# Fewer POOL taps in the second half's conv, more of its steps early, and weights split three chunks ahead

## The chip, the cores and the metric

The kernel runs on one core of one Trainium2 chip. The time is the device time of one launch in microseconds (us); before the change the median of three runs is 1130.25 us (1129.55 to 1130.99). Engines are called as in the profile: PE multiplies matrices, PEld loads its weights, DVE (vector), ACT (scalar, with function tables) and POOL (GpSimd) work elementwise, SP issues transfers. Each engine takes its instructions in one fixed order, and a waiting instruction holds those behind it.

## The reference, cut to what matters

Two layers on 512 tokens of 1024 channels. The change lies in the first, a conv module with an FFN behind it:

```python
a = jax.nn.glu(x @ w_pw1 + b_pw1, axis=-1)
y = lax.conv_general_dilated(
    a, w_dw[:, None, :].astype(a.dtype), window_strides=(1,),
    padding=((CONV_WIDTH - 1, 0),), dimension_numbers=('NWC', 'WIO', 'NWC'),
    feature_group_count=D_MODEL) + b_dw
y = jax.nn.silu(layernorm(y, ln_g, ln_b))
return y @ w_pw2 + b_pw2
```

So each channel of `a` is filtered with its own 31 taps over the current and the 30 tokens before it, the result is normalised over the channels and projected. The FFN is `(silu(gate) * up) @ w_down` on the RMS-normalised sum, with 2816 hidden channels. The second layer is windowed attention and another FFN, and a last norm follows.

## The kernel before, in words

Channels lie on the 128 partitions (8 channel tiles, KT), tokens along the free dimension. The first layer's conv is done in two halves of 256 tokens, so that the conv of one half, elementwise work, can run beside matmuls of the other.

**First projection** (`Pw1`, L555): for each half and channel tile 8 matmuls for the linear part and 8 for the gate, in fp32, each recorded as two. `gate` (L564 on ACT, L569 on DVE) writes the result to `a_pad`.

**Conv** (`Half.taps`, L594 to L608): the 31 taps of a channel tile are divided. N_POOL of them go the POOL way: ACT multiplies a shifted view by the tap (L594, L596) into one of 8 `pr` buffers, and POOL adds it to the running sum (L597). The others go the DVE way: a fused multiply and add into a PSUM bank (L602, L604), the last one into `y`. POOL then adds its sum to `y` (L608). Two channel tiles run side by side as a pair and share one PSUM bank; a step is one DVE tap of each with the POOL taps that fall to it. A pair with n POOL taps has 31 - n tap steps and one step that closes it. The halves have their own N_POOL, given by pair.

**Norm of the conv**: `squares` (DVE L631, ACT L633), `sums` (matmuls with ones, L642), `scales_a` (a copy on ACT, L647, small matmuls, L650, and four small DVE instructions, L652 to L657), `scales_b` (POOL L663, ACT L668), `spread` (PE L672), `rows` (DVE L684 and L685, ACT silu L686).

**Second projection and FFN** (`pw2`, `ffn_part`): their weights come as chunks of 128 x 1024 elements, one per `get`: 8 chunks of pw2, then 24 of the FFN's first part upwards and 12 downwards for one half of the tokens. A chunk is loaded into a `raw` buffer by SP (4 of them, six chunks ahead). The first half's pw2 uses it as it is, in fp32 (L253). All later chunks are split in `advance`: ACT rounds them to `whi` (L203), DVE subtracts for `wlo` (L204), and `mm3` does three matmuls for each pair of tiles (L255 to L257): 24 per chunk. Activations are split in the same way (L375 and L376 for the norm's input, L379 and L380 for the hidden layer). `whi` and `wlo` have 3 buffers each, and a chunk is split two gets ahead of its use. The FFN's RMS norm adds squares up on POOL (L333), sums them on PE (L343), takes the power on POOL (L347), makes a diagonal on ACT (L355) and spreads it on PE (L368). The first use of its result is the evacuation of hidden pairs (L454, L457 on DVE).

**Order.** The program is written as one sequence, and a planner puts each engine's instructions in order by its own estimate of times: of those that are ready in its estimate the one written first goes first. `issue_after(ins)` keeps what is traced inside it behind `ins` on the engine of `ins`. The second half's conv and norm is a generator (`Half.background`) that the first half's work drives: N_EARLY steps of it are taken in the 11th to 14th of the late projections (`at_` 10 to 13), and the rest is a job: `pace`, called in every `get`, takes as many steps as are due at that chunk, linearly over 42 chunks from the first half's second projection on. In the 12th projection (`at_` 11) the sums of the first half's last pair are traced behind the projection's matmuls.

Of the kernel before, what the change touches and what calls it, by code (L numbers as in the profile page):

```python
# [21 lines left out]
KT = D // P  # L22
# [11 lines left out]
HALVES0 = ((0, 6), (6, 11))  # L34
HALVES1 = ((0, 6), (6, 9))
LAST = (9, 11)
N_POOL = ((13, 13, 12, 12), (17, 17, 17, 17))

Q_HEADS = [g * 8 + s * 4 + j for g in range(2) for j in range(4) for s in range(2)]
HEAD_COLS = np.concatenate([np.arange(h * HD, (h + 1) * HD) for h in Q_HEADS])  # L40
# [109 lines left out]
def hybrid_trunk(ctx: ExitStack, tc: tile.TileContext, xT, W, prm_in, wdw_in, sinks, relb, onehot, outT):  # L150
    nc = tc.nc
    cpool = ctx.enter_context(tc.tile_pool(name="const", bufs=1))
    quads = ctx.enter_context(tc.tile_pool(name="quads", bufs=11))
    wpool = ctx.enter_context(tc.tile_pool(name="wts", bufs=3))
    tmp = ctx.enter_context(tc.tile_pool(name="tmp", bufs=5))
    small = ctx.enter_context(tc.tile_pool(name="small", bufs=4))
    ps = ctx.enter_context(tc.tile_pool(name="ps", bufs=8, space=PSUM))
# [8 lines left out]
    def bank():  # L166
        return ps.tile([P, 512], F32, tag="bank", name=uid("bank"))
# [4 lines left out]
    def temp():  # L172
        return tmp.tile([P, 512], F32, tag="tmp", name=uid("tmp"))
# [3 lines left out]

    stream = {"dma": 0, "split": 0, "use": 0}
    raws, splits = {}, {}
    DMA_AHEAD, SPLIT_AHEAD = 6, 2  # L180
    lo_engine = [nc.vector]

    def load(upto):
# [22 lines left out]

    jobs, background, rate, seen = [], [], [0], [0]

    def job(gen, n, g0, g1):
        jobs.append([gen, n, g0, g1, 0])  # L210

    def pace():
        g = seen[0] = seen[0] + 1
        for j in list(jobs):
            while j[4] < j[1] * (g - j[2]) / (j[3] - j[2]):
                j[4] += 1
                if next(j[0], "end") == "end":
                    jobs.remove(j)
                    break
# [17 lines left out]
    def get(*key):  # L237
        advance()
        pace()
        due[0] += rate[0]  # L240
        tick(int(due[0]))
        due[0] -= int(due[0])
        i = stream["use"]
        assert PLAN[i] == key, (PLAN[i], key)
        stream["use"] += 1
        hi, lo = splits.pop(i)
        n = {"kv": 4, "up": 4}.get(key[0], 2)
        sh = dict(a=n)
        return tuple(w and w.rearrange("p (a b) -> p a b", **sh) for w in (hi, lo))
# [53 lines left out]
    ones_m = cpool.tile([P, P], F32, tag="ones_m", name="ones_m")  # L303
# [220 lines left out]
    nc.gpsimd.memset(inv_s, -1.0 / 256)  # L524
    W2 = 256
    N_RAW = 2
    N_EARLY = (7, 3, 4, 2)
    raw = [x[:, HALF[1]] for x in xg]
    for i in range(KT):
        nc.vector.tensor_scalar(raw[i], h[i][:, HALF[0]], col("mix0", i), None, op0=ALU.mult)  # L530
# [3 lines left out]
    def norm_x(rms, tok, pb=None):  # L534
        pb = rms.spread() if pb is None else pb
        for i in range(KT):
            nc.vector.scalar_tensor_tensor(xg[i][:, tok], h[i][:, tok], col("mix0", i), pb,
                                           op0=ALU.mult, op1=ALU.mult)
        return pb

    with tc.tile_pool(name="conv", bufs=2) as cv:
# [29 lines left out]
        class Half:  # L571
            def __init__(self, hf, after=()):
# [3 lines left out]
                self.st = None  # L576
                self.n_steps = sum(TAPS - n + 1 for n in N_POOL[hf]) + KT + 7

            def taps(self, ct, c):
                n_pool = N_POOL[self.hf][ct // 2]  # L580
                a = a_pad[ct][:, self.hf * W2:(self.hf + 1) * W2 + PAD]
                yt = self.y[:, ct, :]

                def tap(j):
                    return wdw[:, ct, j:j + 1]

                nd = TAPS - n_pool
                acc, pi = None, 0
                for i in range(nd):
                    while pi * nd < n_pool * (i + 1):  # L590
                        j = nd + pi
                        pr = cv.tile([P, W2], F32, tag="pr", name=uid("pr"), bufs=8)
                        if acc is None:
                            on_act = nc.scalar.activation(pr, a[:, j:j + W2], AF.Identity, scale=tap(j), bias=col("bdw", ct))  # L594
                        else:
                            on_act = nc.scalar.mul(pr, a[:, j:j + W2], tap(j))  # L596
                            on_pool = nc.gpsimd.tensor_add(pr, acc, pr)  # L597
                        acc = pr
                        pi += 1
                    src = a[:, i:i + W2]  # L600
                    if i == 0 and ct < 4:
                        nc.vector.tensor_scalar(c, src, tap(i), None, op0=ALU.mult)  # L602
                    else:
                        on_dve = nc.vector.scalar_tensor_tensor(yt if i == nd - 1 else c, src, tap(i),  # L604
                                                                c if i else self.shift, op0=ALU.mult, op1=ALU.add)
                    yield
                self.last = on_act.ins, on_dve.ins, on_pool.ins
                nc.gpsimd.tensor_add(yt, yt, acc)  # L608
# [27 lines left out]
            def sums(self, p):  # L636
                if self.st is None:
                    self.st = bank()
                for e in range(2):
                    ct = 2 * p + e  # L640
                    for f, t in enumerate((self.y[:, ct, :], self.sq[e])):
                        nc.tensor.matmul(self.st[:, f * W2:(f + 1) * W2], ones_m, t,  # L642
                                         start=ct == 0 and f == 0, stop=ct == KT - 1 and f == 1)

            def scales_a(self):
                row = temp()
# [44 lines left out]
            def background(self):  # L691
# [3 lines left out]
                for p in range(KT // 2):  # L695
                    for s in range(TAPS - N_POOL[self.hf][p] + 1):
                        next(gen)
# [47 lines left out]
        h0 = Half(0)  # L745
        n_taps = sum(TAPS - n + 1 for n in N_POOL[0])
        taps = h0.conv()
# [20 lines left out]
        follow = {2: [rms1.step1, table_in], 4: [lambda: norm_x(rms1, HALF[1]), h0.shift_rows], 6: [table]}  # L768
        for p, at_ in enumerate((5, 7, 9, 10)):
            follow.setdefault(at_, []).append(lambda p=p: h0.squares(p))  # L770
            follow.setdefault(at_ + 1, []).append(lambda p=p: h0.sums(p))
        follow[11].append(h0.scales_a)
        done, early, late = 0, 0, None
        for at_, (hf, ct) in enumerate(projs):
            if at_ == 13:
                with tc.issue_after(proj.last[1]):
                    spread = h0.spread()
            with tc.issue_after(spread) if at_ == 13 else nullcontext():
                proj = Pw1(hf, ct)
            if late is not None:  # L780
                with tc.issue_after(proj.last[0]):
                    late.gate()
                    gated = late.sig
            late = proj if hf else None
            if hf == 0:
                proj.gate()
                last_sig = proj.sig
            while done < n_taps * min(1, (at_ + 1) / 11):
                next(taps, None)
                done += 1  # L790
            for f in follow.get(at_, ()):
                with tc.issue_after(last_sig) if f is table else nullcontext(), tc.issue_after(proj.last[1 if f == h0.scales_a or at_ < 11 else 0]):
                    f()
            if at_ == 10:
                h1 = Half(1, h0.last)
                second = h1.background()
            if at_ >= 10:

                with ExitStack() as st:
                    for ins in (gated, h0.copied if at_ == 11 else None, h0.varied if at_ == 11 else None, h0.spreads if at_ >= 12 else None):  # L800
                        if ins is None:
                            continue
                        st.enter_context(tc.issue_after(ins))
                    for _ in range(N_EARLY[at_ - 10]):
                        next(second)
                        early += 1
            if at_ == 11:
                h0.scales_b()
# [3 lines left out]
            late.gate()  # L812
        h1.after = [h0.silu]
        base = seen[0]
        job(second, h1.n_steps - early, base, base + 42)
        x0 = {"ffn0": Act(KT)}
        bc0 = new_bc()
        n0 = Next(("ffn0",), x0, bc0, HALF[0])
# [8 lines left out]
    def read_bias():  # L827
        for h0_ in range(0, NH, 2):
            yield
            nc.sync.dma_start(bias[:, h0_:h0_ + 2, :],  # L830
                              bass.AP(tensor=fd.tensor, offset=fd.offset + 127 + h0_ * 3 * P,
                                      ap=[[NH * 3 * P - 1, P], [3 * P, 2], [1, BAND]]))

    base = seen[0]
    job(read_bias(), 9, base, base + 30)
    n1 = Next(("ffn0",), x0, bc0, HALF[1])
    pw2(h1.z, n1)
    ffn_part(0, 0, x0["ffn0"], HALF[1], n1.rms)
# [11 lines left out]
    if True:  # L850
# [20 lines left out]
        for half in range(2):  # L871
# [7 lines left out]
            if half == 0:  # L879
                rs_bc = rms.step2()  # L880
                rs = rms.rs
                for m in range(2):
                    t = temp()
# [4 lines left out]
        for n in range(4):  # L888
            t = temp()
# [258 lines left out]
```

## Time and profile before

| | before |
|---|---|
| median of three runs | 1130.25 us |
| profiled execution | 1130.66 us |
| its span in the trace | 1128.9 us |
| granted TensorE clock, mean | 0.996 |
| busy: PE | 1103.1 us (98%) |
| busy: PE's weight loads | 960.1 us (85%) |
| busy: DVE | 660.7 us (59%) |
| busy: ACT | 515.0 us (46%) |
| busy: POOL | 334.6 us (30%) |

The span is the profiled execution from its first to its last instruction; 1.76 us of its own time lie around it. Busy shares are means over the whole span; the stages differ. In the trace the second projection of the first half begins at 131.3 us, its FFN at 161.35 us, and the second half's own projection and FFN follow from about 265 us. Rows of groups give the line, engine, operation, shapes and count, then the busy time, the mean of one in ns, and the idle time just before with what ended it.

### The profile page before, as it was taken

To read this page: it belongs to the slowest core of one execution; us is meant where nothing else is said; L and a number is where in the kernel's file an instruction comes from. 1 tells how busy PE (TensorE), PEld (TensorE's weight loads), DVE (VectorE), ACT (ScalarE), POOL (GpSimd) and SP (SyncE) were. 2 spreads that over 40 slices of the span, in tenths; PEclk is the share of its full clock that TensorE was granted. 3 is DMA by queue.
4 is the path that set the end of the run, shared out by engine and by line. 5 is a ranking of instruction groups with operands and counts; after the bars stand their busy time and mean duration, and the time that the engine had idled before them with its cause. 6 is when DMAs were issued, how large, how long until landed. Compare 5 with 4: busy or idle time off the path is not lost.

```text
span 1128.9 us, 16125 instructions
## 1 busy us (share of the span) xinstructions
PE 1103.1 (98%) x6140; PEld 960.1 (85%) x6140; DVE 660.7 (59%) x1060; ACT 515.0 (46%) x910; POOL 334.6 (30%) x437
## 2 busy tenths in 40 slices
PE   8999998899999999999999999999999999999997
PEld 7888887899999998888888777888888888888886
DVE  4998868877765554444464685764454333444355
ACT  3886787856454432332352564653232221222234
POOL 3999699930010001111220232231121100110014
PEclk9999999999999999999999999999999999999998
DMA  9227053466555552323223211123223322232222
GB/s 357 100 31 83 23 181 114 137 204 223 184 179 180 187 167 98 106 91 96 93 85 102 76 38 38 38 61 108 93 93 99 106 94 94 93 100 103 96 96 92
DMA packets 41722, 128.16 MB, mean 114 GB/s; under 512 B 4491, under 2 KB 12844, under 8 KB 41644
## 3 DMA queue, kind: packets, MB, share of 16 engines
q1 hardware_dynamic: 40924, 126.56, 35.7%
q8 instruction: 48, 0.79, 0.3%
q10 hardware_dynamic: 720, 0.57, 0.2%
q14 instruction: 30, 0.25, 0.1%
HBM read 121.87 MB, written 5.24 MB: 113 GB/s over the span
## 4 chain that ended last, share of the span: by engine, by line
PE 85%; DVE 5%; issue 5%; POOL 2%; ACT 2%; DMA 1%; SPq 0%; POOLq 0%; ACTq 0%; DVEq 0%
PE bank L255 24%; PE bank L256 24%; PE bank L257 24%; PE bank L555 8%; POOL pr L597 2%; PE bank L919 1%; DVE bank L604 1%; PE bank L940 1%; DVE quad L376 1%; PE bank L642 1%; DVE wlo L204 1%; ACT whi L203 1%; DMA h<-in_xT_dram 1%; ACT pr L596 0%; DVE sc L922 0%
## 5 line engine op out<-in xcount | busy, mean ns | idle before, releaser
L257 PE MATMUL bank<-quad,wlo 128*128 128x512 f32 (+1 forms) x1584 | 542.4, 343 | 4.5 <-DVE wlo L204 4.5
L256 PE MATMUL bank<-quad,whi 128*128 128x512 f32 (+1 forms) x1584 | 542.6, 343 | 2.4 <-DVE quad L376 2.4
L255 PE MATMUL bank<-quad,whi 128*128 128x512 f32 (+1 forms) x1584 | 542.7, 344 | 0.8 <-ACT whi L203 0.6
L204 DVE TENSOR_TENSOR wlo<-raw,whi 128x1024 fp32r<-128x1024 f32 x200 | 271.4, 1357 | 326.0 <-ACT whi L203 317.6
L203 ACT CAST whi<-raw 128x1024 fp32r<-128x1024 f32 x200 | 209.6, 1048 | 357.8 <-PE bank L256 306.5
L257 PEld LDWEIGHTS bank<-quad,wlo 128*128 128x128 f32 x1584 | 299.9, 189 | 40.4 <-DVE wlo L204 6.0
L256 PEld LDWEIGHTS bank<-quad,whi 128*128 128x128 f32 x1584 | 300.2, 189 | 38.2 <-DVE quad L376 3.4
L255 PEld LDWEIGHTS bank<-quad,whi 128*128 128x128 f32 x1584 | 300.0, 190 | 37.1 <-ACT whi L203 0.8
L465 POOL TENSOR_TENSOR tmp<-tmp,tmp 128x512 f32<-128x512 f32 x32 | 45.6, 1427 | 485.0 <-DVE tmp L464 471.5
L597 POOL TENSOR_TENSOR pr<-pr,pr 128x256 f32<-128x256 f32 x220 | 170.5, 812 | 14.0 <-ACT pr L596 13.7
L596 ACT ACTIVATE pr<-apad,wdw 128x256 f32<-128x256 f32 x220 | 105.3, 503 | 27.1 <-POOL pr L597 25.3
L555 PE MATMUL bank<-quad,w 128*128 128x256 f32 x512 | 113.4, 380 | 2.3 <-DMA w<-in_W_dram 1.3
L555 PEld LDWEIGHTS bank<-quad,w 128*128 128x128 f32 x512 | 96.6, 190 | 17.3 <-DVE quad L530 4.1
L604 DVE SCALAR_TENSOR_TENSOR bank<-apad,wdw,bank 128x256 f32<-128x256 f32 x236 | 108.5, 485 | 3.6
L333 POOL TENSOR_TENSOR tmp<-tmp,tmp 128x256 f32<-128x256 f32 (+1 forms) x42 | 44.4, 1057 | 133.4 <-ACT tmp L329 109.4
L463 ACT ACTIVATE tmp<-tmp 128x512 f32<-128x512 f32 x32 | 20.1, 632 | 86.4 <-DVE tmp L462 86.4
L933 POOL TENSOR_SCALAR sc<-sc,sm 128x256 f32<-128x256 f32 (+1 forms) x64 | 30.8, 503 | 86.1 <-DVE sm L931 86.0
L379 ACT CAST quad<-tmp 128x512 fp32r<-128x512 f32 (+1 forms) x48 | 27.9, 585 | 29.7 <-POOL tmp L465 25.8
L376 DVE SCALAR_TENSOR_TENSOR quad<-h,prm,quad 128x512 fp32r<-128x512 f32 (+1 forms) x40 | 39.2, 1011 | 1.9 <-ACT quad L375 1.7
L464 DVE TENSOR_TENSOR tmp<-bank,rsbc 128x512 f32<-128x512 f32 x32 | 22.1, 691 | 30.4 <-PE bank L257 30.4
L929 ACT ACTIVATE sc<-sc,m 128x257 f32<-128x257 f32 (+1 forms) x64 | 30.2, 475 | 15.2 <-DVE m L922 14.5
L380 DVE TENSOR_TENSOR quad<-tmp,quad 128x512 fp32r<-128x512 f32 (+1 forms) x48 | 31.0, 650 | 2.3 <-ACT quad L379 2.3
(137 smaller groups left out, 749.7 us busy)
## 6 DMA issues: line engine op xcount, KB each, us to landing
raw<-in_W_dram SPq DMA_DIRECT2D x208, 512.0 KB, 3.5
w<-in_W_dram SPq DMA_DIRECT2D x15, 512.0 KB, 9.6
fd<-fs SPq DMA_DIRECT2D x1, 3072.0 KB, 33.8
h<-in_xT_dram SPq DMA_DIRECT2D x8, 256.0 KB, 6.6
bias<-fd SPq DMA_DIRECT2D x8, 256.0 KB, 7.8
out_dram<-res SPq DMA_DIRECT2D x13, 128.0 KB, 1.8
w<-in_W_dram SPq DMA_DIRECT2D x2, 256.0 KB, 4.4
out_dram<-res ACTq DMA_DIRECT2D x3, 128.0 KB, 2.4
```

The costliest lines, as they stand in the source:

```text
L203: nc.scalar.copy(hi, r)
L204: lo_engine[0].tensor_sub(lo, r, f32(hi))
L255: nc.tensor.matmul(out, w[0], x[0], start=start, stop=False)
L256: nc.tensor.matmul(out, w[0], x[1], start=False, stop=False)
L257: nc.tensor.matmul(out, w[1], x[0], start=False, stop=stop)
L333: self.eng.tensor_add(sq, self.acc, sq)
L376: nc.vector.scalar_tensor_tensor(dst[1], src, g, f32(dst[0]), op0=ALU.mult, op1=ALU.subtract)
L465: nc.gpsimd.tensor_mul(t2, t1, t2)
L555: mm = nc.tensor.matmul(self.pb[:, w * W2:(w + 1) * W2], w1[ct][:, w, k, :], x[k] if x else xg[k][:, tok], start=k == 0, stop=k == KT - 1)
L596: on_act = nc.scalar.mul(pr, a[:, j:j + W2], tap(j))
L597: on_pool = nc.gpsimd.tensor_add(pr, acc, pr)
L604: on_dve = nc.vector.scalar_tensor_tensor(yt if i == nd - 1 else c, src, tap(i), c if i else self.shift, op0=ALU.mult, op1=ALU.add)
```

## The change

Four edits. In the second half's conv the pairs 2 to 4 have 15 POOL taps instead of 17, so 16 DVE taps instead of 14. The four late projections take 8, 4, 5 and 3 steps of that conv instead of 7, 3, 4 and 2, and the job's due steps are now a broken line: 20 steps within the first 8 chunks (the second projection), the rest evenly up to chunk 42. The sums of the first half's last pair are traced between the linear and the gate half of the 12th projection, and the gate half is kept behind them. Weights are split three gets ahead instead of two, with 4 buffers for `whi` and `wlo` each.

```diff
-N_POOL = ((13, 13, 12, 12), (17, 17, 17, 17))
+N_POOL = ((13, 13, 12, 12), (17, 15, 15, 15))
...
-    wpool = ctx.enter_context(tc.tile_pool(name="wts", bufs=3))
+    wpool = ctx.enter_context(tc.tile_pool(name="wts", bufs=4))
...
-    DMA_AHEAD, SPLIT_AHEAD = 6, 2
+    DMA_AHEAD, SPLIT_AHEAD = 6, 3
...
-    def job(gen, n, g0, g1):
-        jobs.append([gen, n, g0, g1, 0])
+    def job(gen, *points):
+
+        jobs.append([gen, points, 0])
+
+    def due_at(points, g):
+        for (g0, n0), (g1, n1) in zip(points, points[1:]):
+            if g <= g1:
+                return n0 + (n1 - n0) * (g - g0) / (g1 - g0)
+        return 1 << 30
...
-            while j[4] < j[1] * (g - j[2]) / (j[3] - j[2]):
-                j[4] += 1
+            while j[2] < due_at(j[1], g):
+                j[2] += 1
...
-    N_EARLY = (7, 3, 4, 2)
+    N_EARLY = (8, 4, 5, 3)
...
-        follow[11].append(h0.scales_a)
+        follow[11] = [h0.scales_a]
...
-                proj = Pw1(hf, ct)
+                proj = Pw1(hf, ct, mid=(lambda: h0.sums(3)) if at_ == 11 else None)
...
-        job(second, h1.n_steps - early, base, base + 42)
+        job(second, (base, 0), (base + 8, 20), (base + 42, h1.n_steps - early))
...
-    job(read_bias(), 9, base, base + 30)
+    job(read_bias(), (base, 0), (base + 30, 9))
```

`sums` now returns its last matmul, behind which `Pw1` puts the gate half (`with tc.issue_after(mid()) if w and mid`); the bias job keeps its line.

More of the change, by code (lines that the diff above doesn't have):

```diff
@@ L641, in sums @@
                     for f, t in enumerate((self.y[:, ct, :], self.sq[e])):
-                        nc.tensor.matmul(self.st[:, f * W2:(f + 1) * W2], ones_m, t,
-                                         start=ct == 0 and f == 0, stop=ct == KT - 1 and f == 1)
+                        mm = nc.tensor.matmul(self.st[:, f * W2:(f + 1) * W2], ones_m, t,
+                                              start=ct == 0 and f == 0, stop=ct == KT - 1 and f == 1)
+                return mm.ins
             def scales_a(self):
```

## The prediction

> **What bounds the kernel now.** I began with the page's busy times and slices.
>
> ```profile
> span 1128.9 us, 16125 instructions
> ...
> PE 1103.1 (98%) x6140; PEld 960.1 (85%) x6140; DVE 660.7 (59%) x1060; ACT 515.0 (46%) x910; POOL 334.6 (30%) x437
> ...
> POOL 3999699930010001111220232231121100110014
> ```
>
> PE bounds the program; only stretches in which PE waits can give time back. POOL is full in slices of 28 us between about 28 and 240 us and nearly idle afterwards, and that is where the conv lies that the change edits. So I read next what PE waited for from 150 to 480 us: waits in total, their number, the longest.
>
> ```profile
> PE bank L257 <- DVE wlo L204: 4.5, 5, 1.3
> PE bank L368 <- ACT tmp L355: 1.8, 1, 1.8
> PE bank L256 <- DVE quad L376: 1.5, 2, 0.9
> PE bank L343 <- POOL tmp L333: 1.1, 1, 1.1
> PE bank L650 <- ACT tmp L647: 0.7, 1, 0.7
> PE bank L255 <- ACT whi L203: 0.6, 1, 0.6
> ```
>
> All but the 0.7 fall between 161 and 240 us, beside the first half's FFN: 9.5 us in 10 waits. A wait costs a little more than its idle time:
>
> ```profile
> 214.91 0.28 PE L255 MATMUL bank<-quad,whi 128*128 128x256 f32 x1
> 215.03 0.28 PE L256 MATMUL bank<-quad,whi 128*128 128x256 f32 x1
> 216.31 0.39 PE L257 MATMUL bank<-quad,wlo 128*128 128x256 f32 x1 [0.99 <-DVE wlo L204]
> ```
>
> Neighbours start 0.12 us apart, here it is 1.28: 1.16 us are lost for 0.99 idle. With 0.17 us for each of the 10, the stage loses **11.2 us**; that is all this stage can give. A weight chunk of 24 matmuls is 24 x 0.12 = 2.88 us of PE.
>
> Why is the weight split (L203 on ACT, then L204 on DVE) late? The chain of waits just before the last of these stalls (start, us, what):
>
> ```profile
> 219.68 1.58 issue
> 221.26 0.73 POOL pr L597
> ...
> 222.07 2.42 POOL pr L597 x2
> ...
> 224.94 1.04 ACT whi L203
> ...
> 226.01 1.68 DVE wlo L204
> ...
> 227.73 0.39 PE bank L257
> ```
>
> The chain runs along POOL's tap additions, over to ACT and DVE, and so to PE. ACT's queue is in order: a product (L596) that waits for one of eight `pr` buffers, which only POOL's addition frees, holds the split queued behind it. From 161.4 to 240 us:
>
> ```profile
> ACT pr L596 <- POOL pr L597: 10.5, 16, 1.9
> DVE wlo L204 <- ACT whi L203: 9.4, 9, 1.9
> ```
>
> POOL has no gap between 138.61 and 233.7 us. Ahead of that it has two (timeline of POOL: start, us, count, idle before):
>
> ```profile
> 116.15 2.79 POOL L597 TENSOR_TENSOR pr<-pr,pr 128x256 f32<-128x256 f32 x4 [4.37 <-ACT pr L596]
> ...
> 119.58 9.68 POOL L597 TENSOR_TENSOR pr<-pr,pr 128x256 f32<-128x256 f32 x14
> ...
> 138.61 10.73 POOL L597 TENSOR_TENSOR pr<-pr,pr 128x256 f32<-128x256 f32 x15 [7.99 <-ACT pr L596]
> ```
>
> **POOL's work, and what the change takes from it.** An undisturbed addition is 9.68/14 = 0.69 us. In the full stretch (groups from 138.6 to 233.8 us; POOL, then DVE):
>
> ```profile
> L597 POOL TENSOR_TENSOR pr<-pr,pr 128x256 f32<-128x256 f32 x94 | 83.4, 921 | 8.3 <-ACT pr L596 8.0
> ```
> ```profile
> L204 DVE TENSOR_TENSOR wlo<-raw,whi 128x1024 fp32r<-128x1024 f32 x21 | 33.4, 1592 | 15.6 <-ACT whi L203 15.6
> ```
>
> The 94 took 83.4 - 94 x 0.69 = 18.5 us more than undisturbed, while DVE did 21 wlo subtractions: 0.88 us for each. Where POOL is idle (280 to 400 us) the subtraction itself is shorter:
>
> ```profile
> L204 DVE TENSOR_TENSOR wlo<-raw,whi 128x1024 fp32r<-128x1024 f32 x42 | 51.3, 1224 | 36.3 <-ACT whi L203 36.1
> ```
>
> So each makes the other wait, and POOL's loss goes with the number of splits, not with the number of additions.
>
> The change drops from 17 to 15 POOL taps for six of eight channel tiles: 12 additions and 12 products fewer, 12 more DVE taps. The early steps (N_EARLY) rise from 16 to 20. The first pair of tiles takes 15 steps, so five steps of the second pair come early instead of one: 10 products and 8 additions instead of 4 and 2. Those 6 additions can run in the gaps of 4.37 and 7.99 us. The stretch loses 18 additions: 18 x 0.69 = **12.4 us**; ends: 12 x 0.69 = 8.3 us if the early ones find no room, 18 x 0.92 = 16.6 us if each is worth the mean. I take 0.69 since the splits that lengthen the others remain. The Trainium skill, "SBUF — State Buffer", section "Who interferes with whom", states that a VectorE instruction with two SBUF inputs and a GpSimd instruction that reads SBUF hold one shared port by turns, each for its whole length, while one SBUF input does not contend. By that rule 12.4 stands (L204 reads two SBUF tiles, a tap one tile and a PSUM bank); by the group's mean alone it would be 16.6. The trace agrees with the rule: 1.22 against 1.59 us for L204.
>
> Is POOL then early enough? Before, 59 job steps are spread over 42 chunks, and the last tap step is the 44th: chunk 31.3, that is 23.3 after the 8 of the second projection. the FFN starts here:
>
> ```profile
> 161.35 0.47 PE L255 MATMUL bank<-quad,whi 128*128 128x256 f32 x1
> ```
>
> PE reaches the last tap step at 161.35 + 23.3 x 2.88 = 228.5 us if nothing stalls; POOL is done at 233.7, about 5 us late. After, 20 steps come in the first 8 chunks and the last tap step is the 46th: chunk 8 + 26 x 34/41 = 29.6, PE at 222.7 us; POOL at 233.7 - 12.4 = 221.3. It is **no longer late**. Splitting three chunks ahead, with a fourth pair of buffers, adds cover: a split is asked for one chunk, 2.88 us, earlier, and the longest split wait is 1.3. The split waits (4.5 + 0.6 us in 6 waits, 6.1 with the restarts) should mostly go.
>
> **DVE is the next.** Busy times by stage (us; PE, PEld, DVE, ACT, POOL):
>
> ```profile
> 131.30:161.35 30.05, 30.05 (x141) 26.43 (x141) 18.22 (x40) 23.89 (x51) 22.74 (x31) 1.00 0.38 122
> 161.35:190.00 28.65, 24.20 (x186) 22.92 (x185) 24.81 (x39) 21.83 (x46) 28.65 (x31) 1.00 0.45 149
> 190.00:237.30 47.30, 42.07 (x328) 39.95 (x328) 42.38 (x60) 38.43 (x68) 43.41 (x46) 1.00 0.45 148
> ```
> ```profile
> L604 DVE SCALAR_TENSOR_TENSOR bank<-apad,wdw,bank 128x256 f32<-128x256 f32 x48 | 23.1, 481 | 0.6
> ```
>
> In the FFN's 75.95 us DVE has 67.2 us of work (88%). Without stalls the same PE work takes 75.95 - 11.2 = 64.8 us, so DVE would be the bound there unless work leaves the stage. In program order 52 of 112 taps were due by the end of the second projection; after, 76 of 124. So 48 instead of 60 remain: 12 x 0.481 = 5.8 us less, and one split (1.59) falls earlier: 59.8 of 64.8 us. The 24 taps that move need 11.5 us, and DVE has 30.05 - 18.22 = 11.8 us free beside the second projection. It just fits, so I don't expect all of the 6.1 us back: I take 70%, **4.3 us**; ends 2.0 and 6.1. On ACT 12 products fewer are no gain of their own; its waits are POOL's.
>
> **The other terms.** The sums of the first half's last pair move between the two halves of the 12th projection. Now PE does 32 matmul records, then the sums, then waits:
>
> ```profile
> 106.19 7.07 PE L555 MATMUL bank<-quad,w 128*128 128x256 f32 x32
> 113.09 0.59 PE L642 MATMUL bank<-y,ones_m 128*128 128x256 f32 x2
> ...
> 115.66 1.05 PE L650 MATMUL bank<-ident,tmp 128*128 128x1 f32 x8 [0.68 <-ACT tmp L647]
> ```
> ```profile
> 106.75 0.40 ACT L633 ACTIVATE sq<-y 128x256 f32<-128x256 f32 x1
> ```
>
> The squares are done at 107.15; half of the projection ends at 106.19 + 6.9/2 = 109.6. So the sums run 3.45 us earlier, the copy (L647) is hidden behind the projection's other half, and the wait with its restart, **0.8 us**, goes; ends 0 and 0.8. Four early steps more are 8 DVE taps ahead of the first half's normalised rows, but DVE ran taps of those very steps there already, and it idles 5.43 us while PE does the sums:
>
> ```profile
> 116.75 0.16 DVE L652 TENSOR_SCALAR mv<-bank 128x2 f32<-128x2 f32 x1 [5.43 <-PE bank L650]
> ```
>
> So I let the rows move with PE. The first four waits of the FFN (1.8 + 1.5 + 1.1 us, 5.1 with restarts) are start-up: the norm's sum on POOL, its scale, the split of x on DVE. One wlo subtraction fewer stands among the x splits; I take **0.6 us** off, ends -2.5 (a loss) and +2.5, because the planner may order these queues anew. After 480 us PE's longest wait is the tail's, and none is for a weight split (L203, L204):
>
> ```profile
> PE bank L1072 <- DVE tmp L1062: 1.5, 1, 1.5
> PE bank L256 <- DVE ptl L944: 1.3, 2, 0.7
> ```
>
> So three chunks ahead bring nothing there; the new orders are worth 0, ends 0.6 either way. Raw loads get no slower: one buffer less is held between load and split.
>
> Sum: 0.8 + 4.3 + 0.6 = 5.7 us. The profiled execution took 1130.66 us (1128.9 in the span, 1.76 around it), so it would take 1125.0; it stands 0.41 above the median of the three runs, 1130.25, for which I say **1124.5 us**.
>
> **Rivals.** *A, DVE takes POOL's place.* If the third pair of tiles gets no PSUM bank for its sums before the second projection ends (before, DVE stood idle there in a gap of 6.20 us although taps were left), the 24 taps don't move: DVE's stage load is 67.2 + 5.8 - 1.6 = 71.4 us, and at 94% density that is 76 us, what the stage takes now. Only the 0.8 us stay: 1129.5. The row that speaks for it:
>
> ```profile
> 156.69 1.64 DVE L204 TENSOR_TENSOR wlo<-raw,whi 128x1024 fp32r<-128x1024 f32 x1 [6.20 <-ACT whi L203]
> ```
>
> Against it: the third pair's first step is the 13th of the job instead of the 15th, and at 20 steps in 8 chunks it is asked for at chunk 6 instead of 11.
> *B, slower: the norm's sum queues behind the pulled-forward taps.* POOL does 31 operations beside the second projection. After the change 47 are due there if the early ones find no room: the second pair's 30, 14 of the third, 3 of the norm (L333). The 16 left behind may stand ahead of the four L333 that complete the FFN's norm, the last of which runs here:
>
> ```profile
> 177.41 0.72 POOL L333 TENSOR_TENSOR tmp<-tmp,tmp 128x256 f32<-128x256 f32 x1
> ```
>
> Six tap additions stand between those four now, so 10 are new: 10 x 0.92 = 9.2 us in which PE waits at L343. It decides once that last L333 ends more than 6 us later than now against the FFN's start; fully paid it gives 1124.5 + 9.2 = 1133.7. Against it: 8 of the 16 fit the gaps of 4.37 and 7.99 us, and the additions interleave with taps today at equal load.
> *C, all stalls go:* 0.8 + 11.2 = 12 us, 1118.2. Against it: the start-up chain POOL, DVE, ACT, PE is a dependence, not a queue alone.
>
> **Chances.** Forecast 0.62, A 0.18, B 0.09, C 0.11. A measurement can tell about 0.2% (2.3 us) from no change. The forecast's own range by the ends is 0.8 + 2.0 - 2.5 - 0.6 to 0.8 + 6.1 + 2.5 + 0.6, near 0 to 10 us, mostly over 2.3; so faster 0.58 of 0.62 plus C plus a little of A: 0.72; same 0.20; slower 0.08, nearly all B. The range, 1119.5 to 1131.5, takes in the forecast, A and the milder part of C.
>
> **What would show it.** Right: no 0.7 wait at L650; POOL's full stretch ends near 221 us and ACT's waits for `pr` fall well under 10.5; PE's waits for wlo fall from 4.5 to about 1; DVE's gap of 6.20 is filled with taps. Wrong: POOL still full until 230 us (12.4 mis-sized), DVE over 95% in the FFN with PE waiting on L204 or L376 (A), or PE's wait at L343 or L368 grown by several us (B).

## The result, and the profile after

The changed kernel takes 1122.53 us (median of five runs, 1121.57 to 1123.15), the kernel before 1129.66 us on the same chip. The ratio is 0.9929 with a 95% interval of 0.9918 to 0.9941: between 0.6% and 0.8% faster. The forecast was 1124.5. The profiled execution took 1122.53 us, its span is 8.2 us shorter. Three rows of its page:

```profile
span 1120.7 us, 16124 instructions
...
PE 1103.7 (98%) x6140; PEld 963.7 (86%) x6140; DVE 663.5 (59%) x1072; ACT 509.2 (45%) x898; POOL 324.0 (29%) x425
...
POOL 3999699810200001211230232241111100110014
```

POOL has 12 instructions fewer and DVE 12 more, and POOL's slices between about 170 and 250 us read 9, 8, 1 instead of 9, 9, 3. (Seven lines were added ahead of the conv, so L255 to L257 are now L262 to L264, L333 is L340, L343 is L350, L368 is L375, L376 is L383, L597 is L604, L604 is L611, L608 is L615, L642 is L649; with one more, L647 is L655 and L650 is L658.) What PE waits for from 150 to 480 us, the view that had six rows and 10.2 us:

```profile
PE bank L350 <- POOL tmp L340: 3.1, 1, 3.1
PE bank L263 <- DVE quad L383: 0.9, 3, 0.4
```

All waits for weight splits are gone (5.1 us before), so are the waits for the spread of the norm's scale (1.8) and for the copy of the conv's sums (0.7). One wait has grown, from 1.1 to 3.1 us: that for the FFN norm's sum. And something new stands behind it. PE's timeline there (start, us, operation, idle before):

```profile
178.58 0.61 PE L350 MATMUL bank<-ones_c,tmp 128*128 128x1 f32 x4 [3.10 <-POOL tmp L340]
...
179.36 0.28 PE L264 MATMUL bank<-quad,wlo 128*128 128x256 f32 x1
179.48 0.28 PE L262 MATMUL bank<-quad,whi 128*128 128x256 f32 x1
...
180.22 0.42 PE L264 MATMUL bank<-quad,wlo 128*128 128x256 f32 x1
180.44 0.41 PE L262 MATMUL bank<-quad,whi 128*128 128x256 f32 x1
```

From 0.12 us apart the same matmuls go to 0.22. The windows' column of the granted clock (the third from the right) tells why:

```profile
179.90:183.30 3.40, 3.40 (x18) 3.40 (x18) 1.37 (x3) 2.20 (x4) 3.40 (x5) 0.50 0.35 102
```

For 3.41 us TensorE runs at half its clock, which costs about 1.7 us. In the profiled execution of the kernel before there was no such stretch in this stage.

POOL's timeline has the gap at 111 to 116 us closed, and the full stretch now runs from 139.42 to 219.6 us, 80.2 us instead of 95.1:

```profile
105.78 12.42 POOL L604 TENSOR_TENSOR pr<-pr,pr 128x256 f32<-128x256 f32 x18
...
139.42 9.83 POOL L604 TENSOR_TENSOR pr<-pr,pr 128x256 f32<-128x256 f32 x14 [9.59 <-ACT pr L603]
...
192.81 26.80 POOL L604 TENSOR_TENSOR pr<-pr,pr 128x256 f32<-128x256 f32 x27
```

The groups in that stretch, POOL and then DVE:

```profile
L604 POOL TENSOR_TENSOR pr<-pr,pr 128x256 f32<-128x256 f32 x76 | 69.1, 943 | 9.6 <-ACT pr L603 9.6
```
```profile
L204 DVE TENSOR_TENSOR wlo<-raw,whi 128x1024 fp32r<-128x1024 f32 x18 | 27.9, 1548 | 10.3 <-ACT whi L203 10.2
```

94 additions became 76. What the additions take beyond 0.69 us comes to (69.1 - 76 x 0.69) / 18 = 0.93 us per split, 0.88 before. The trace shows directly that it is paid per split: sorted by what DVE did at the same time, the 31 additions that overlap a split (L204) take 1.22 us on average, and the 38 that overlap neither a split nor the split of x (L383) take 0.73 us, none of them more than 0.75 (0.69 from start to start).

### The profile page after: what moved, and what is told of

The parts are those of the page before. It is cut to its first block, busy times and chain, and to the rows that moved or that the text cites. A ratio compares the mean times of both kernels' runs of the same rounds, so it can differ in the third digit from the quotient of the medians.

```text
span 1120.7 us, 16124 instructions
## 1 busy us (share of the span) xinstructions
PE 1103.7 (98%) x6140; PEld 963.7 (86%) x6140; DVE 663.5 (59%) x1072; ACT 509.2 (45%) x898; POOL 324.0 (29%) x425
## 4 chain that ended last, share of the span: by engine, by line
PE 90%; DVE 3%; ACT 3%; issue 2%; POOL 1%; DMA 1%; POOLq 0%; SPq 0%; ACTq 0%; DVEq 0%
PE bank L262 26%; PE bank L263 26%; PE bank L264 25%; PE bank L562 9%; PE bank L927 1%; PE bank L649 1%; PE bank L948 1%; ACT pr L603 1%; POOL pr L604 1%; DVE quad L383 1%; ACT whi L203 1%; DVE wlo L204 0%; DVE bank L611 0%; DVE sc L930 0%; DMA raw<-in_W_dram 0%
## 5 line engine op out<-in xcount | busy, mean ns | idle before, releaser
L262 PE MATMUL bank<-quad,whi 128*128 128x512 f32 (+1 forms) x1584 | 543.8, 345 | 0.2
L264 PE MATMUL bank<-quad,wlo 128*128 128x512 f32 (+1 forms) x1584 | 542.9, 343 | 0.0
L204 DVE TENSOR_TENSOR wlo<-raw,whi 128x1024 fp32r<-128x1024 f32 x200 | 269.3, 1347 | 318.2 <-ACT whi L203 310.1
L262 PEld LDWEIGHTS bank<-quad,whi 128*128 128x128 f32 x1584 | 300.7, 190 | 36.5 <-ACT quad L966 0.6
L264 PEld LDWEIGHTS bank<-quad,wlo 128*128 128x128 f32 x1584 | 300.9, 190 | 34.5 <-DVE wlo L204 0.2
L604 POOL TENSOR_TENSOR pr<-pr,pr 128x256 f32<-128x256 f32 x208 | 160.5, 822 | 11.0 <-ACT pr L603 11.0
L611 DVE SCALAR_TENSOR_TENSOR bank<-apad,wdw,bank 128x256 f32<-128x256 f32 x248 | 113.2, 485 | 3.5
L562 PEld LDWEIGHTS bank<-quad,w 128*128 128x128 f32 x512 | 98.5, 193 | 14.9 <-DVE quad L537 0.9
L603 ACT ACTIVATE pr<-apad,wdw 128x256 f32<-128x256 f32 x208 | 99.6, 503 | 23.8 <-POOL pr L604 21.7
L340 POOL TENSOR_TENSOR tmp<-tmp,tmp 128x256 f32<-128x256 f32 (+1 forms) x42 | 45.2, 1076 | 135.2 <-ACT tmp L336 111.1
L383 DVE SCALAR_TENSOR_TENSOR quad<-h,prm,quad 128x512 fp32r<-128x512 f32 (+1 forms) x40 | 39.4, 1020 | 0.5 <-ACT quad L382 0.4
```

The costliest lines, as they stand in the source:

```text
L204: lo_engine[0].tensor_sub(lo, r, f32(hi))
L262: nc.tensor.matmul(out, w[0], x[0], start=start, stop=False)
L264: nc.tensor.matmul(out, w[1], x[0], start=False, stop=stop)
L340: self.eng.tensor_add(sq, self.acc, sq)
L383: nc.vector.scalar_tensor_tensor(dst[1], src, g, f32(dst[0]), op0=ALU.mult, op1=ALU.subtract)
L562: mm = nc.tensor.matmul(self.pb[:, w * W2:(w + 1) * W2], w1[ct][:, w, k, :], x[k] if x else xg[k][:, tok], start=k == 0, stop=k == KT - 1)
```

## The experiments

The prediction's theory, called L in the expectations, is that PE waits for splits because POOL is late and ACT's order hands that on. Twelve kernels were run. "Only" means the kernel before with one part of the change; "without" means the changed kernel with one part taken back. Beside the ratio to the kernel before I give two sums from each profile: PE's idle time between 95 and 270 us, and the time at half clock ahead of the tail. Both come from one execution of each kernel.

| kernel | ratio (95%) | PE idle, us | half clock, us |
|---|---|---|---|
| before | 1 | 11.0 | 0 |
| changed | 0.9929 (0.9918 to 0.9941) | 4.0 | 3.4 |
| only the taps | 0.9986 (0.9976 to 0.9995) | 8.3 | 6.8 |
| only the splits | 0.9981 (0.9972 to 0.9991) | 7.9 | 3.4 |
| only the steps | 1.0022 (1.0012 to 1.0032) | 11.1 | 10.2 |
| without the splits | 0.9959 (0.9944 to 0.9974) | 6.0 | 3.4 |
| without the taps | 0.9971 (0.9960 to 0.9982) | 6.7 | 3.4 |
| without the steps | 0.9944 (0.9928 to 0.9960) | 5.4 | 3.4 |
| without the moved sums | 0.9950 (0.9935 to 0.9965) | 5.5 | 3.4 |
| norm's additions on DVE | 0.9934 (0.9919 to 0.9949) | 4.7 | 3.4 |
| norm's sum a chunk later | 0.9958 (0.9943 to 0.9973) | 5.7 | 3.4 |
| last two squares summed by PE | 0.9945 (0.9928 to 0.9961) | 4.8 | 3.4 |
| last four squares summed by PE | 0.9945 (0.9931 to 0.9960) | 3.7 | 3.4 |
| norm ahead of the taps | 0.9907 (0.9891 to 0.9924) | 3.1 | 3.4 |

The half clock doesn't come equally often in every execution. The mean granted clock of the kernel before is 0.994 in ten of the 25 runs beside the first experiments and 0.996 or 0.997 in the rest; its profile has 0.996 with 8.4 us of half clock, all in the tail. A mean of 0.994 takes over 12 us of it, so by this estimate those ten had a stretch earlier too. And each edit makes the planner order all engines anew; no run here changes one part and keeps the order, so how much of a difference of 1 or 2 us is the part and how much the order stays open.

**Only the taps.**

```diff
-N_POOL = ((13, 13, 12, 12), (17, 17, 17, 17))
+N_POOL = ((13, 13, 12, 12), (17, 15, 15, 15))
```

> The kernel before with only the POOL taps of pairs 2 to 4 changed from 17 to 15 (12 additions fewer on POOL, 12 taps more on DVE). Theory L (PE's waits for weight splits are POOL's lateness, handed on by ACT's order): POOL's full stretch, 138.6 to 233.7 us, ends some 8 us earlier (12 x 0.69), the waits of PE for wlo and whi fall from 5.1 us to 1 to 2, and the time falls by about 4 us, to 1126. Theory S (the split is simply asked for too late; POOL's load matters little): the waits for wlo stay between 4 and 5 us and the time stays within 1 us of before.

Less than half of the 4 us expected by L: 0.14%, 1.6 us. POOL's stretch ends at 226.4 us, 7.4 us earlier, as L says. PE's waits from 95 to 270 us:

```profile
PE bank L257 <- DVE wlo L204: 2.4, 3, 1.1
PE bank L642 <- POOL y L608: 2.2, 1, 2.2
...
PE bank L255 <- ACT whi L203: 0.4, 1, 0.4
```

The split waits fell from 5.1 to 2.8 us as L says, though not to 1 or 2. But a wait of 2.2 us for POOL's last addition of a pair (L608) is new. It is the third pair's: with more tap steps it closes later, at 211.3 us instead of 201.1, and the planner puts its sums (L642) later too, but not by as much (290 weight-split matmuls behind the FFN's start instead of 242, and 48 are 5.8 us at 0.12). And two stretches at half clock appear, some 3.4 us lost, which neither theory had.

**Only the splits.**

```diff
-    wpool = ctx.enter_context(tc.tile_pool(name="wts", bufs=3))
+    wpool = ctx.enter_context(tc.tile_pool(name="wts", bufs=4))
...
-    DMA_AHEAD, SPLIT_AHEAD = 6, 2
+    DMA_AHEAD, SPLIT_AHEAD = 6, 3
```

> The kernel before with only the splits three chunks ahead and four buffers for whi and wlo. Theory L: POOL is late as before (full until about 231 us), one chunk of cover (2.88 us) takes about half of the 6.1 us of split waits: about 3 us faster, 1127. Theory S: all split waits go: 6 us faster, 1124, with POOL's stretch still as full as before.

```profile
PE bank L257 <- DVE wlo L204: 3.3, 6, 1.1
PE bank L650 <- ACT tmp L647: 2.0, 2, 1.3
PE bank L343 <- POOL tmp L333: 1.7, 1, 1.7
PE bank L256 <- DVE quad L376: 0.9, 2, 0.6
```

These are PE's waits from 95 to 270 us in this kernel. By the medians it is 2.2 us faster. S falls: with one chunk more of cover, 3.3 of the 5.1 us of split waits stay. L's "about half" was a little too much.

**Only the steps.**

```diff
...
-    N_EARLY = (7, 3, 4, 2)
+    N_EARLY = (8, 4, 5, 3)
...
-        job(second, h1.n_steps - early, base, base + 42)
+        job(second, (base, 0), (base + 8, 20), (base + 42, h1.n_steps - early))
```

(`job` and `pace` change with it, as in the whole diff.)

> The kernel before with only the earlier steps (8, 4, 5, 3 beside the late projections, then 20 within the first 8 chunks). Theory L: about 6 additions move out of the full stretch, 4 us less on POOL there, about 2 us faster; the gap of 6.2 us on DVE at 150 to 157 us is filled. Theory S: no change within 1 us. If pulled-forward taps delay the FFN's norm, PE's wait for POOL before the norm's sum grows from 1.1 us to 3 or more, and the time stays or grows.

L's 2 us of gain didn't come: 2.2 us slower by the medians, with an interval wholly above 1. PE's waits, and two windows behind the longest of them:

```profile
PE bank L649 <- POOL y L615: 3.8, 1, 3.8
PE bank L264 <- DVE wlo L204: 3.0, 3, 1.2
PE bank L375 <- ACT tmp L362: 1.8, 1, 1.8
PE bank L350 <- POOL tmp L340: 1.5, 1, 1.5
```
```profile
222.00:224.90 2.90, 0.99 (x9) 0.78 (x7) 2.81 (x3) 0.34 (x1) 2.90 (x2) 1.00 0.26 78
224.90:231.80 6.90, 5.00 (x21) 4.82 (x22) 2.52 (x3) 2.77 (x5) 2.53 (x4) 0.51 0.41 135
```

Not the norm's sum (1.5 us) but the conv's last sums are what PE waits for here, 3.8 us. POOL ends the first of that pair's last additions at 226.7 us, 12 us earlier than before (238.6), but the planner puts the sums 386 weight-split matmuls behind the FFN's start instead of 576, and 190 matmuls are 23 us at 0.12. The 10.2 us at half clock cost about 4.2 us, since PE stood idle in 1.8 of them. A part of a change that helps in company costs time alone.

**Without the splits, without the taps, without the steps.** Each is one of the three diffs above, taken back from the changed kernel.

> The changed kernel with splits two chunks ahead and three buffers, as before. Theory L (POOL no longer late, so the cover is hardly used): at most 1 us slower than the changed kernel, 1123 to 1124, PE's waits for wlo under 1 us. Theory J (fewer taps and earlier steps only set the stage, and PE's order is written for a POOL that real time doesn't follow; the extra chunk is what absorbs that): waits for wlo or whi of 3 to 5 us return, 1126 to 1128.

> The changed kernel with 17 POOL taps in all pairs. Theory L: POOL's stretch is full until about 228 us again, about 4 us slower than the changed kernel, 1126 to 1127, and PE waits for POOL's last addition of a pair (y) or for wlo. Additive reading of the runs so far (taps alone gave 1.6 us): 1124.

> The changed kernel with the old early steps (7, 3, 4, 2) and the old even pace. Additive reading (the steps alone cost 2.2 us): 2 us faster than the changed kernel, 1120. If the steps matter because DVE has 12 taps more and needs the room beside the second projection (rival A of the prediction): PE waits for wlo or for sums, 1126 or more, DVE idle again for some 5 us between 150 and 157 us.

Without the splits PE waits 1.9 us for wlo and whi again and at both ends of the norm's chain; the ratio is higher by 0.0030 (3.4 us), its interval just above the changed kernel's. That is a larger loss than L's 1 us, with less than J's 3 to 5 us of waits. Without the taps the loss is the largest, 0.42% (0.9971 against 0.9929), 4.7 us, near L's 4:

```profile
PE bank L350 <- POOL tmp L340: 3.5, 1, 3.5
PE bank L264 <- DVE wlo L204: 1.5, 2, 1.1
PE bank L658 <- ACT tmp L655: 1.2, 1, 1.2
```
```profile
197.17 30.24 POOL L604 TENSOR_TENSOR pr<-pr,pr 128x256 f32<-128x256 f32 x30
227.37 1.44 POOL L615 TENSOR_TENSOR y<-y,pr 128x256 f32<-128x256 f32 x2
```

POOL is full until 227.4 us, as L said (228). But with POOL as late as that only 1.5 of the 5.1 us of split waits are back, and the profiled execution, at 1124.86 us, is the fastest of this kernel's seven: it and one more (1125.07) have a mean clock of 0.996, the other five take 1126.1 to 1127.7 us at 0.992 or 0.993. So part of the 4.7 us goes with more time at half clock. Without the steps the interval overlaps the changed kernel's: no loss can be told, and no gain, so the additive reading falls. DVE does stand idle beside the second projection there, but PE's waits for wlo are only 0.4 us:

```profile
154.50 1.62 DVE L204 TENSOR_TENSOR wlo<-raw,whi 128x1024 fp32r<-128x1024 f32 x1 [5.52 <-ACT whi L203]
```

**Without the moved sums.** The sums of the first half's last pair stand behind the whole 12th projection again.

```diff
-        follow[11] = [h0.scales_a]
+        follow[11].append(h0.scales_a)
...
-                proj = Pw1(hf, ct, mid=(lambda: h0.sums(3)) if at_ == 11 else None)
+                proj = Pw1(hf, ct)
```

> The changed kernel with the sums of the first half's last pair behind the whole projection, as before. By the prediction's term: PE's wait at the copy of the sums (0.68 us, 0.8 with the restart) comes back at about 115 us, 0.8 us slower than the changed kernel, 1123.3. If the earlier sums also set the early steps going (they wait for the copy), POOL's pause of 4.4 us at 112 to 116 us comes back too and POOL ends later: 1 to 3 us slower.

The wait of 0.68 us is back and POOL's pause at 115 us with 3.0 us, but POOL's stretch ends no later (219.3 us, 219.6 in the changed kernel), which the second case had expected; the ratio rises by 0.0021, but the intervals overlap, so its size stays open between nothing and some 4 us.

**The wait that has grown.** Five kernels tried to remove the 3.1 us at the norm's sum.

```diff
...
+                self.rms.eng = self.eng or nc.gpsimd
...
+        n0.eng = nc.vector
```

> The changed kernel with one edit more: the additions of squares for the first half's FFN norm (7 of 128x256) run on DVE instead of POOL. If PE's wait of 3.1 us at the norm's sum is POOL's queue, it falls under 1 us; if the 3.41 us at half the TensorE clock that follow are a consequence of that wait, they go as well: 3.1 + 1.7, about 4 to 5 us faster than the changed kernel, 1118. If the granted clock falls for another reason, the half-clock stretch stays and the gain is 3 us at most. If DVE's load is the limit there, PE waits for x (quad) or wlo instead, and the time stays at about 1122.

Here the norm's additions (L340) run on DVE. No wait at the sum is left, yet the time is the changed kernel's: PE waits 2.3 us for x (L383), 1.3 for wlo and 1.0 for the spread, and a half-clock stretch comes at 170.3 us.

```diff
+                    if half == 0 and which == 0 and pending:
+                        rms.step1()
...
             if w == 256 and pair == lo:
-                rms.step1()
```

> The changed kernel with the FFN norm's sum on PE traced one chunk (2.88 us) later, for both halves. If the 3.1 us wait at that sum is only its place in PE's order, it falls to about 0.5 us, and if the half-clock stretch after it follows from the wait, that goes too: 3 to 4 us faster than the changed kernel, 1118 to 1119. If the norm's chain (POOL, DVE, POOL, ACT, PE) is what everything behind it depends on, the wait comes back at the spread of the scale (ACT tmp) and the time stays within 1 us of 1122.

The wait moved, as the second case says, but the time didn't stay within 1 us: 1124.62 us, with an interval (0.9943 to 0.9973) just above the changed kernel's. 0.3 us are left at the sum, and then

```profile
PE bank L375 <- ACT tmp L362: 4.6, 1, 4.6
```

The chain of waits shows what the scale's power (L354) waits for: POOL does conv additions (L605 in this kernel) between the norm's last addition and the power.

```profile
181.40 0.60 issue
182.00 0.09 POOL pr L605
...
183.40 1.73 POOL pr L605
...
186.43 0.72 POOL pr L605
187.16 1.66 POOL rs L354
...
188.84 0.04 ACT tmp L362
...
189.59 1.22 PE bank L375 x2
```

The next two leave the last two, or four, of the eight squares to PE's sum.

```diff
-            for i in range(n):
-                nc.tensor.matmul(st[:, i:i + 1], self.acc[:, i * P:(i + 1) * P], ones_c, start=i == 0, stop=i == n - 1)
+            parts = [self.acc] + self.rest
+            for a, part in enumerate(parts):
+                for i in range(n):
+                    nc.tensor.matmul(st[:, i:i + 1], part[:, i * P:(i + 1) * P], ones_c,
+                                     start=a == 0 and i == 0, stop=a == len(parts) - 1 and i == n - 1)
...
+        n0.n_sum = 6
```

> The changed kernel, in which the last two of the eight squares of the first half's FFN norm aren't added up by POOL but go to PE's sum as they are (4 small matmuls more, 0.5 us on PE; 2 additions fewer on POOL). If PE's wait of 3.1 us at the sum is the last two additions' place in POOL's queue, it falls below 1 us and the half-clock stretch after it goes: 3 to 4 us faster than the changed kernel, 1119. If the power on POOL and the diagonal behind it hold the chain, the wait comes back at the spread (ACT tmp): within 1 us of 1122.5.

> The same with the last four squares (8 small matmuls more, 1 us on PE; 4 additions fewer on POOL, which then has only the tap additions of this stretch in its queue ahead of the power). Queue reading: no wait at the sum, the power comes earlier as well, a gain of 3 to 4 us, 1119. Chain reading: the wait at the spread stays, 1122 to 1123.

No wait at the sum is left in either, but with two squares 3.9 us came back at the spread, with four 1.3 us there and 1.3 us at a wlo. Neither gains: 1124.07 and 1124.25 us. So with two squares it is POOL's queue ahead of the power that PE waits for: the planner puts 14 conv additions between the norm's last addition and the power, 6 in the changed kernel. The last kernel therefore fixes POOL's order itself: no conv step is due in the FFN's first four chunks, and later additions are kept behind the norm's last addition and behind the power.

```diff
+    hold = []
...
                 rms.step1()
+                for a in hold:
+                    a.append(rms.power)
+                hold.clear()
...
+        hold.append(h1.after)
...
-        job(second, (base, 0), (base + 8, 20), (base + 42, h1.n_steps - early))
+        job(second, (base, 0), (base + 8, 20), (base + 12, 20), (base + 42, h1.n_steps - early))
...
+        h1.after.append(n0.rms.last_add)
```

> The changed kernel, in which POOL does the FFN norm's last additions and its power ahead of the conv additions of later steps: no conv step is due in the FFN's first four chunks, and later additions are kept behind the norm's last addition and, once it is traced, behind the power. If the 3.1 us wait at the norm's sum (and the 3.9 to 4.6 us that came back at the spread in two other kernels) is POOL's queue, which holds the norm's additions and its power behind conv additions, both waits fall below 1 us together and no half-clock stretch follows: 3 to 5 us faster than the changed kernel, 1118 to 1119. If the conv work that is pushed back by some 12 us overloads DVE or POOL later (both are about 90% busy from 190 to 230 us), PE's waits for wlo come back with 2 to 5 us and the time is 1121 to 1124.

1119.82 us, ratio 0.9907: the fastest kernel here. Neither the sum nor the spread is waited for. In POOL's timeline the power (L355 in this kernel) stands right behind the norm's additions (L341), with idle time ahead of it; the second fence has PE's waits from 100 to 480 us:

```profile
175.56 2.54 POOL L341 TENSOR_TENSOR tmp<-tmp,tmp 128x256 f32<-128x256 f32 x2
179.53 0.71 POOL L355 TENSOR_TENSOR rs<-ms,mhalf 128x2 f32<-128x2 f32 x1 [1.43 <-DVE ms L353]
180.21 13.56 POOL L608 TENSOR_TENSOR pr<-pr,pr 128x256 f32<-128x256 f32 x14
```
```profile
PE bank L264 <- DVE quad L384: 1.5, 1, 1.5
PE bank L263 <- ACT quad L383: 0.9, 1, 0.9
PE bank L265 <- DVE wlo L204: 0.6, 1, 0.6
```

DVE carries the pushed-back work without a stall: 29.75 of 30 us busy from 200 to 230 us. But new waits of 3.0 us stand before 172 us, 2.4 at the split of x and 0.6 at a weight split, and a half-clock stretch follows these as well. The gain over the changed kernel is 2.5 us by the ratios and not 3 to 5, and by the intervals, 0.9891 to 0.9924 and 0.9918 to 0.9941, it is likely but not beyond doubt.

Counted from the FFN's start (159.94 us in the changed kernel, 159.65 here), the two profiles show that this gain is not the wait at the sum. POOL's last norm addition ends 18.6 us after that start in the changed kernel and 18.5 us here; PE comes to the sum after 18.6 and 19.1 us. The sum isn't waited for here because PE, held up by the new waits and the half clock, comes to it later. POOL does end the power earlier, after 20.6 instead of 25.4 us, but the spread behind it was not waited for in the changed kernel either. Between the 100th and the 200th weight-split matmul, behind the sum, this kernel then gains 1.5 us: in the changed kernel the half-clock stretch lies there, and here it lies ahead of the sum, where PE would otherwise have waited for POOL. The two profiled executions differ by 1.5 us (1122.53 and 1121.07); what makes x late here isn't shown.

## Why the prediction was right, and where it was off

- *POOL loses 12.4 us of its full stretch.* Right in kind: 18 additions fewer, as counted. It lost 14.9 us, between the 12.4 taken and the end of 16.6: a shorter stretch also holds fewer splits (18 instead of 21), each of which holds POOL up by 0.9 us. That the loss goes with the splits and not with the additions is shown by the additions' own times, 1.22 us beside a split and 0.73 elsewhere. The Trainium skill, "SBUF — State Buffer", section "Who interferes with whom", states that a VectorE instruction with two SBUF inputs contends with a GpSimd instruction that reads SBUF; these times agree.
- *POOL done at 221.3 us, PE there at 222.7; the split waits should mostly go: 4.3 us.* POOL was done at 219.6, and all 6.1 us went. The 70% was the mis-sized term. It rested on DVE having 59.8 of 64.8 us to do; by the windows it was busy 21.06 + 36.86 = 57.9 us in the 69.5 us from 160.5 to 230:

```profile
160.50:190.00 29.50, 25.54 (x184) 24.22 (x183) 21.06 (x26) 22.57 (x46) 29.50 (x31) 0.94 0.49 158
190.00:230.00 40.00, 40.00 (x326) 39.52 (x325) 36.86 (x53) 29.23 (x51) 31.98 (x32) 1.00 0.52 170
```

  DVE ran ahead of the steps' due places: by the FFN's start 89 of the 124 taps are done, where the prediction counted 76 as due, and the third pair's last tap ends at 163.8 us. Two of its counts were off by a step. The job takes its 12th step at the eighth chunk (8 x 59/42 = 11.2 are due), so 54 taps and not 52 were due before. And the 44th and 46th steps are those that close the last pair; the last tap steps are the 43rd and 45th, which PE reaches some 2 us earlier than the prediction said, so that by its own sum POOL (221.3) would still have been 1 us late. The waits went even so. DVE's timeline of the changed kernel shows the gap of 6.20 us filled:

```profile
151.20 3.63 DVE L611 SCALAR_TENSOR_TENSOR bank<-apad,wdw,bank 128x256 f32<-128x256 f32 x7
155.43 1.64 DVE L204 TENSOR_TENSOR wlo<-raw,whi 128x1024 fp32r<-128x1024 f32 x1 [0.60 <-ACT whi L203]
```

- *Rival A, DVE takes POOL's place:* fell, by these rows. Even without the steps, where the gap stays, PE hardly waits for wlo.
- *The moved sums: 0.8 us.* The wait went. The run without them confirms the place; POOL's pause, which comes back there, shows what the prediction left out, that the early steps wait for the same copy. The same wait at the second half's sums (0.68 us at 250.5 us) went as well, another 0.8 us that was not in the sum.
- *The FFN's start-up: 0.6 us off.* Here the step failed in its sign. The waits fell from 4.4 to 4.0 us of idle time, but the half clock behind the sum took 1.7 us, a term the prediction didn't have, so the start-up became some 1.3 us longer. Rival B's mechanism is there in small: the first of the last four L340 begins 9.1 us after the FFN's start instead of 7.3 (L333 before), with POOL busy up to it, and against the FFN's start the last L340 ends at 178.53 - 159.94 = 18.6 us instead of 178.13 - 161.35 = 16.8 us, 1.8 us later, below B's point of 6. With it the wait at the sum grew to 3.1 us.
- *The parts taken one by one.* The prediction added up terms. The runs show that the parts don't add: alone they give 0.14%, 0.19% and -0.22%, together with the moved sums 0.71%. In each of the three the planner made a new order, in which PE waits elsewhere (for `y`, for the copy of the sums), and by the profiles the half clock took back 1.7 to 4.2 us. That these two add up to the shortfall isn't shown.
- The forecast of 5.7 us met 7.1 us by the medians: missing were 1.8 us of split waits and 0.8 us at the second sums; too much was 0.2 us at the start-up, and the half clock's 1.7 us was not foreseen. That leaves 0.7 us, of which 0.5 is there in the profiles by 22 us, ahead of all that the change touches (PE's waits for the first weights); the rest is not assigned. So the nearness of 1124.5 to 1122.5 is in part luck: missed gains and a missed loss made up for each other.

## What to carry to other kernels

Where an engine off the critical path is full, its lateness reaches PE through whatever queue stands between; count what is queued behind a wait, and per what the engine loses time (here per split, 0.9 us, not per addition). Relief of that engine and cover for its users belong together: each alone was worth a fifth to a quarter of the whole. When a wait moves instead of going away, as that for the norm did in four kernels, look for what the waits have in common. Ordering the engine that they came from made the fastest kernel here, though PE did not come to the sum any earlier by it: a wait that is no longer listed may only have been spent elsewhere, so compare when the work behind it starts.

## What the runs showed that I had not expected

TensorE's clock falls to half for stretches of 3.41 us, or twice that, shortly after PE has waited, also where the wait is shorter than the stretch. In the changed kernel it followed a wait of 3.10 us, in the kernel with only the steps one of 1.79 us, and in the last kernel waits of 0.85 and 1.47 us some 3 us apart:

```profile
172.50:175.80 3.30, 3.30 (x16) 3.11 (x15) 3.30 (x3) 2.63 (x6) 3.30 (x4) 0.50 0.05 19
```

In the kernel before, a wait of 1.77 us, as long as that of 1.79, brought none. What tells the two apart is where the wait lies. In each of the 14 profiles every change of the granted clock stands a whole number of times 3.413 us behind the clock's first rise (in the changed kernel the rise is at 9.23 us and the fall at 179.90, 50 times 3.413 later). So the traces do show the borders of the windows by which the clock is set. Laid on them, first the kernel before and then the kernel with only the steps (window; length, PE's busy time; the granted clock is again the third from the right):

```profile
181.80:185.21 3.41, 2.85 (x24) 2.64 (x23) 2.05 (x3) 2.66 (x5) 3.41 (x5) 1.00 0.38 144
185.21:188.63 3.42, 2.21 (x17) 2.16 (x17) 2.53 (x4) 2.84 (x6) 3.42 (x5) 1.00 0.42 156
```
```profile
184.00:187.41 3.41, 1.62 (x12) 1.36 (x12) 3.14 (x5) 2.33 (x6) 3.41 (x5) 1.00 0.29 60
187.41:190.83 3.42, 3.42 (x19) 3.42 (x18) 2.86 (x4) 2.60 (x6) 3.42 (x4) 0.50 0.42 125
```

The wait of 1.77 us is cut by a border into 0.56 and 1.21 us; that of 1.79 us lies in one window, and the next one runs at half clock. Between 95 and 270 us the profiles have 15 falls. In 13 of them PE was idle for 1.6 us or more of the window just before, and of the windows at full clock that no fall followed one had 1.85 us idle and all others under 1.5. (In the kernel with only the steps a half-clock window in which PE was idle for 1.8 us is followed by a second one.) The other two falls came behind windows with 1.3 us idle and four matmuls of one column (only the taps), and with 1.9 us of matmuls of one column and no idle time (last four squares summed by PE), so such matmuls seem to count as little work. About half a window, then, is enough in these profiles; the exact share stays open.

So a wait on PE can cost 1.7 us more than it lasts, and whether it does depends on where the windows lie; the clock's first rise stands anywhere from 4.3 to 9.9 us after the first instruction in these profiles. The Trainium skill, "TensorE: Matmul & The Clock Gate", section "Part 1: The HAM clock gate", states that a free-running window of about 3.4 us without work brings the half clock. The spacing agrees (3.413 us), and two kernels here have a window without any matmul ahead of the fall (norm's sum a chunk later, last two squares summed by PE); in the others less than that was enough.
